# The value product of layer B in plain fp32, two heads side by side in the array's columns

## The chip, the core and the metric

The kernel runs on one core of a Trainium2 chip. The metric is device time in microseconds (us) of one execution. Each compute engine has an instruction stream of its own: TensorE (PE; its weight loads are shown apart as PEld), VectorE (DVE), ScalarE (ACT) and GpSimd (POOL). All transfers of this kernel are issued from SyncE (SP). PE writes its products to PSUM; ACT and DVE read them there; everything else lies in SBUF.

## The reference

Two layers of gated attention over a prompt of 2048 tokens and a sample of 64 tokens, model width 1024, float32 throughout. Layer A has 16 query heads and 2 key/value heads; layer B, where the change is, has 16 heads of 64 columns each. For layer B:

```
h = rms_norm(x, norm_b); q, k, v, gate = split(h @ w_in_b)        # 1024 -> 4 x 1024
q, k = rms_norm per head
s = q k^T / 8 + bias(clipped distance)                            # own chunk of 64 tokens + 8 chunks back
p = softmax(s)
o = p v                                                           # the value product
y = x + (o * silu(gate)) @ w_out_b
```

The sample's 64 tokens attend to 256 cached ones and to themselves. Updated key and value buffers are returned too.

## The kernel before, in words

**Precision.** Large products aren't run in fp32 but in fp32r, a rounded form of it. Each operand is split: a high part (the value rounded to fp32r) and a low part (the value minus its high part). A projection is then three products per weight block: high x high, high x low, low x high. `split_to` (L820) makes such a pair: ACT copies the source into the high part (L822), DVE subtracts (L823).

**Work of layer B.** The prompt is cut into 8 units of 256 tokens (two tiles of 128), the sample is a ninth unit of 64. Heads go in 8 pairs (hp). For each pair and unit, `gen` projects (L529 to L531; the sample L522 to L525), `evacuate` scales the result into SBUF, and `take_vg` hands the values on: `split_v` (L799) writes v's high part by ACT (L801) and its low part by POOL (L802). `VT` holds them for 16 token tiles as [high 64 columns | low 64 columns] per head, `VS` those of the sample.

**Attention of layer B.** For each tile and head, `scores` multiplies queries and keys (L1489, L1490), takes the row maximum with the bias (DVE, L1496) and the exponential (ACT, L1500). `values` (L1519) transposes the probabilities of one tile and head on PE (L850, fp32, against an identity) and splits the result into `ph` and `pl` with `split_to`. `outputs(it, h)` (L1541) is the value product of one head: for each key tile, the stationary operand is the 128 columns [v high | v low] and the moving operand first `ph` (L1566), then `pl` (L1567), added up in PSUM tile `o`. A full unit has four key tiles that all 256 queries see and two that one half sees (128 columns); the first units have fewer. Rows 0 to 63 of `o` then hold high v times p, rows 64 to 127 low v times p. For the second head, `outputs` also transposes the gate on PE, ACT evacuates it (`gate_t`, L1226), and `finish_pairs` (L1229) adds the halves: two ACT copies (L1234), two DVE additions (L1236), a POOL product with the gate (L1237), and a store.

**What sets the order.** PE's order is written out by hand. `pipeline` (L1577) goes through units, and in a unit through four slots (head 0 tile 0, head 0 tile 1, head 1 tile 0, head 1 tile 1). In each slot it emits the scores of this slot, the transposes of the slot before, and, if a head was completed, its value product one slot later. Between these it calls `filler.to(...)`: the filler hands out projection matmuls of later units until a mark is reached, so that PE always has independent work; when layer B's projections are done, it hands out layer B's output projection (L1664 to L1666). The marks count the filler's own columns alone. Work of the other engines is put in a queue (`bg`) with estimated costs and is emitted between; a planner with a simulated timeline orders those engines' streams.

**Fp32 on PE.** Apart from transposes, few fp32 products exist before: the bias vectors (`bias_vectors_a`, L158, 383 columns), and sums of squares against a column of ones (L465, L479).

**Unused code.** `PLAIN = 8` switches off a block scheme for the projections (`block_weights`, `product`, `sums`, `gen_sample`, `gen_blocks`): no head pair reaches it. Its slots in the DRAM cache tensor `xo` stay reserved.

Of the kernel before, what the change touches and what calls it, by code (L numbers as in the profile page):

```python
# [9 lines left out]
F32 = mybir.dt.float32  # L10
# [26 lines left out]
PLAIN = 8  # L37
S_FIRST = (6, 7)
# [17 lines left out]
def hybrid_encoder_kernel(  # L56
# [174 lines left out]
    xo = dr.tile([P, 8 * NU + 1, 8 * P], F32, tag="xo", name="xo")  # L231
# [306 lines left out]
    PIECE = dict(P1="11", P6="T2", P2="21", P7="T3", P5="T1", P4="T4", P3="22")  # L538
    OPERAND = dict(P1="A11", P6="S2", P2="A12", P7="S3", P5="S1", P4="A22", P3="S4")
    SLOT = {n: i for i, n in enumerate(("A11", "A12", "A21", "A22", "S1", "S2", "S3", "S4"))}  # L540

    def block_weights(src):
        w = {n: [Item(), Item()] for n in PIECE.values()}
        raw, todo, emitted = {}, [], []

        def fetch():
            order_ = [(b, a) for b in ("11", "12", "22", "21") for a in range(2)]
            for x, (b, a) in enumerate(order_):
                r = t("wraw", [P, 512], WB) if x < WB else t("xraw", [P, 2 * OT], XR)
                rv = r[:, :512].rearrange("p (k c) -> p k c", k=2)  # L550
                c = 256 * (int(b[1]) - 1)
                held["w"] = load(rv, src[2 * (int(b[0]) - 1) + a][:, :, c : c + 256]).ins
                raw[b, a] = rv

        def g(i, a, j):
            k = 4 * (i - 1) + 2 * a + j
            return gain[:, 1, k : k + 1]

        def piece(n, a, b, scaled):
            def fn():  # L560
                q = w[n][a]
                q.h = wh = t("wh", [P, 1, 512], WN, F32R)[:, 0].rearrange("p (k c) -> p k c", k=2)
                q.l = wl = t("wl", [P, 1, 512], WN, F32R)[:, 0].rearrange("p (k c) -> p k c", k=2)
                rv = raw[b, a]
                if not scaled:
                    nc.scalar.copy(wh, rv)
                    nc.vector.tensor_tensor(wl, rv, wh.bitcast(F32), op=ALU.subtract)
                    return
                for j in range(2):
                    s = g(int(b[0]), a, j)  # L570
                    nc.scalar.activation(wh[:, j], rv[:, j], AF.Identity, scale=s)
                    nc.vector.scalar_tensor_tensor(
                        wl[:, j], rv[:, j], s, wh[:, j].bitcast(F32), op0=ALU.mult, op1=ALU.subtract
                    )
            return 0.8, fn, w[n][a]

        def mix(dst, src_, other, a, op):
            def fn():
                for j in range(2):
                    nc.vector.scalar_tensor_tensor(  # L580
                        raw[dst, a][:, j], raw[src_, a][:, j], g(int(src_[0]), a, j), raw[other, a][:, j],
                        op0=ALU.mult, op1=op,
                    )
            return 0.6, fn, None

        def scaled_12(a):
            def fn():
                for j in range(2):
                    nc.scalar.activation(raw["12", a][:, j], raw["12", a][:, j], AF.Identity, scale=g(1, a, j))
            return 0.6, fn, None  # L590

        two = range(2)
        todo += [piece("11", a, "11", True) for a in two]
        todo += [f(a) for a in two for f in (scaled_12, lambda a: mix("12", "22", "12", a, ALU.subtract))]
        todo += [mix("11", "11", "12", a, ALU.add) for a in two]
        todo += [piece("T2", a, "11", False) for a in two]
        todo += [piece("21", a, "21", True) for a in two]
        todo += [mix("21", "21", "11", a, ALU.subtract) for a in two]
        todo += [piece("T3", a, "12", False) for a in two]
        todo += [mix("11", "22", "11", a, ALU.subtract) for a in two]  # L600
        todo += [piece("T1", a, "11", False) for a in two]
        todo += [piece("T4", a, "21", False) for a in two]
        todo += [piece("22", a, "22", True) for a in two]

        def emit(m=len(todo)):
            if not raw:
                fetch()
            for _ in range(min(m, len(todo))):
                cost, fn, q = todo.pop(0)
                b = bg.put(cost, fn, lazy=filler.n > 0)  # L610
                emitted.append(b)
                if q is not None:
                    q.upto = len(emitted)

        def parts(n, k):
            q = w[n][k // 2]
            for b in emitted[: q.upto]:
                bg.run(b)
            return q.h[:, k % 2], q.l[:, k % 2]

        return parts, emit

    def product(ps, xc, parts, p, start):
        xh, xl = xc.op[OPERAND[p]]
        for k in range(4):
            wh, wl = parts(PIECE[p], k)
            nc.tensor.matmul(ps[:, :256], xh[:, k], wh, start=start and k == 0, stop=False, skip_group_check=not start)
            nc.tensor.matmul(ps[:, :256], xh[:, k], wl, start=False, stop=False, skip_group_check=not start)
            nc.tensor.matmul(ps[:, :256], xl[:, k], wh, start=False, stop=k == 3, skip_group_check=not start)
            if k < 3:  # L630
                yield 3 * 256 / 2400
# [5 lines left out]
    def load_b(unit, hp):  # L637
# [14 lines left out]
        if T == TS:  # L652
            if hp:
                x.joint = cached("J", 8 * NU)[:, : 8 * P].rearrange("p (k s) -> p k s", k=8)
                return x
            raw = t("xraw", [P, 2 * OT], XR)[:, :512].rearrange("p (k s) -> p k s", k=8)
            held["last"] = load(raw, x1[:, :, SEQ:TOK]).ins

            def fn():
                xx = t("xx", [P, 4 * OT], XN, F32R)  # L660
                x.joint = v = xx[:, : 8 * P].rearrange("p (k s) -> p k s", k=8)
                split(xx, v[:, :, :TS], v[:, :, TS:], raw, 8 * NU)

            x.items.append(bg.put(0.52, fn))
            return x
# [11 lines left out]
        def part(n, src, keep):  # L677
            def fn():
                xx = t("xx", [P, 4 * OT], XN, F32R)
                xh, xl = operand(xx)  # L680
                split(xx, xh, xl, raw[src], 8 * u + SLOT[n])
                if keep:
                    x.op[n] = xh, xl
            return fn

        def sums():
            for dst, a, b, op in (
                ("A22", "A21", "A22", ALU.add), ("A21", "A11", "A21", ALU.subtract),
                ("A11", "A22", "A11", ALU.subtract), ("A12", "A12", "A11", ALU.subtract),
            ):  # L690
                def fn(dst=dst, a=a, b=b, op=op):
                    nc.vector.tensor_tensor(raw[dst], raw[a], raw[b], op=op)
                bg.put(0.6, fn)
            for n, src in (("S1", "A22"), ("S3", "A21"), ("S2", "A11"), ("S4", "A12")):
                bg.put(0.52, part(n, src, False))

        if hp == 0:
            raws()
            x.items = [bg.put(0.52, part(n, n, True)) for n in names]
            if u in S_FIRST and PLAIN < 8:  # L700
                sums()
        elif hp < PLAIN:
            for n in names:
                x.op[n] = operand(cached(n, 8 * u + SLOT[n]))
            if u not in S_FIRST and PLAIN < 8:
                raws()
                sums()
        else:
            for n in OPERAND.values():
                x.op[n] = operand(cached(n, 8 * u + SLOT[n]))  # L710
# [120 lines left out]
    def load_cache(ktsrc, vsrc, C, both):  # L831
# [409 lines left out]
    def layer_b():  # L1241
# [4 lines left out]
        def add_unit(hp, unit):  # L1246
# [13 lines left out]
            def weights(*m):  # L1260
                if hp not in st.emit:
                    if hp < PLAIN:
                        (st.w[hp],), _, st.emit[hp] = load_weights(1, (w_in_b[hp], 512))
                    else:
                        st.w[hp], st.emit[hp] = block_weights(w_in_b[hp])
# [40 lines left out]
            def gen_sample():  # L1306
                xc = st.x.pop((hp, u))
                it.prs, it.gate, it.todo = {}, {}, []
                parts = st.w[hp]
                cost = 2 * 256 / 2400  # L1310
                n = TS
# [500 lines left out]
```

## Time and profile before

| what | us |
|---|---|
| median of 3 runs | 2290.27 (2289.32 to 2291.33) |
| the profiled execution, its own time | 2289.07 |
| its span, first to last instruction | 2287.3, mean granted clock of TensorE 0.998 |
| PE busy, all of the span | 2250.9 |
| DVE, ACT, POOL busy | 1539.7, 1466.8, 854.8 |
| 885 to 2072: layer B's attention beside its projections | PE busy 1181.86 of 1187 |
| 2072 to 2130: the rest of it beside the output projection | PE busy 56.60 of 58 |
| 2130 to the end: output projection alone | PE busy 152.53 of 157.3 |

A group row of the profile gives line, engine, operation, tiles (out<-in), array shape (rows * columns of the stationary operand), shape of the moving operand and type, count, then busy time, mean ns of one, and the idle time of the engine just before with what ended it. A timeline row gives start and length in us; merged rows ("x5") give the length of the group. The length of a matmul has a tail that lies under the next one, so lengths don't add up to time; distances between starts do. A wait row gives who waited for whom, the total in us, how many times, and the longest.

### The profile page before, as it was taken

How to read it: one execution, taken by the hardware profiler on the slowest of the kernel's cores; microseconds unless marked ns; L12 is line 12 of the kernel's file. 1: busy time of each engine (PE TensorE's matmuls, PEld its weight loads, DVE VectorE, ACT ScalarE, POOL GpSimd, SP SyncE). 2: the span in 40 equal slices, each digit the busy share in tenths (PEclk: the TensorE clock that was granted, in tenths of full speed). 3: DMA queues.
4: the chain of work that ended last, by engine and by line, in shares of the span. 5: the costliest groups of instructions: out<-in, count | busy, mean ns of one | idle time of the engine just before them, and what ended most of it. 6: DMA issues, size and time to landing. Idle time of an engine off the chain costs nothing. (4 is left out here: it accounts for less than half of the span.)

```text
span 2287.3 us, 41688 instructions
## 1 busy us (share of the span) xinstructions
PE 2250.9 (98%) x13981; PEld 1984.5 (87%) x13981; DVE 1539.7 (67%) x4400; ACT 1466.8 (64%) x3757; POOL 854.8 (37%) x1225
## 2 busy tenths in 40 slices
PE   8999999999999999999999999999999999999999
PEld 7887888888889997888888888888888888888999
DVE  7779888887785545766766766757667667676211
ACT  7888777777773435766666766667667666675321
POOL 5654533333355446442222322322223223234442
PEclk9999999999999999999999999999999999999999
DMA  8846446755437767454454544444445444433664
GB/s 283 296 138 219 161 141 187 227 164 162 147 109 206 213 210 257 160 177 142 150 144 133 156 138 151 136 146 142 142 141 155 138 140 143 137 121 109 194 187 134
DMA packets 236806, 379.31 MB, mean 166 GB/s; under 512 B 24288, under 2 KB 167024, under 8 KB 236560
## 3 DMA queue, kind: packets, MB, share of 16 engines
q1 hardware_dynamic: 236592, 376.65, 53.8%
q8 instruction: 110, 1.80, 0.3%
q14 instruction: 104, 0.85, 0.1%
HBM read 296.13 MB, written 82.08 MB: 165 GB/s over the span
## 5 line engine op out<-in xcount | busy, mean ns | idle before, releaser
L529 PE MATMUL pj<-wh,xx 128*128 128x512 f32 x1024 | 421.9, 412 | 0.0
L531 PE MATMUL pj<-wh,xx 128*128 128x512 f32 x1024 | 403.6, 394 | 0.0
L530 PE MATMUL pj<-wl,xx 128*128 128x512 f32 x1024 | 402.8, 393 | 0.0
L1500 ACT ACTIVATE p<-p,nm 128x640 f32<-128x640 f32 (+5 forms) x272 | 204.2, 751 | 189.4 <-DVE nm L1496 187.7
L1664 PE MATMUL pj<-xx,wh 128*128 128x264 f32 x1024 | 294.4, 288 | 5.2 <-DVE res L1669 5.2
L391 POOL TENSOR_TENSOR xx<-xraw,xx 128x528 fp32r<-128x528 f32 (+1 forms) x168 | 225.1, 1362 | 196.6 <-ACT xx L390 187.1
L1665 PE MATMUL pj<-xx,wh 128*128 128x264 f32 x1024 | 292.0, 285 | 0.0
L1666 PE MATMUL pj<-xx,wl 128*128 128x264 f32 x1024 | 290.6, 284 | 0.0
L823 DVE TENSOR_TENSOR pl<-sb,ph 128x640 fp32r<-128x640 f32 (+5 forms) x272 | 194.8, 716 | 106.0 <-ACT ph L822 102.2
L1496 DVE CUSTOM_DVE_ANT_0 p<-sb,BT 128x640 f32<-128x640 f32 (+5 forms) x272 | 197.0, 724 | 102.0 <-PE sb L1490 99.0
L728 PE MATMUL pj<-wh,xx 128*128 128x512 f32 (+1 forms) x624 | 245.5, 393 | 1.7 <-ACT pb L750 1.2
L729 PE MATMUL pj<-wl,xx 128*128 128x512 f32 (+1 forms) x624 | 232.7, 373 | 2.3 <-DVE wl L320 2.3
L730 PE MATMUL pj<-wh,xx 128*128 128x512 f32 (+1 forms) x624 | 233.4, 374 | 0.0
L531 PEld LDWEIGHTS pj<-wh,xx 128*128 128x128 f32 x1024 | 192.6, 188 | 45.1 <-POOL xx L649 0.4
L1237 POOL TENSOR_TENSOR o<-gt,o 128x256 f32<-128x256 f32 (+2 forms) x140 | 107.8, 770 | 314.8 <-issue 117.9
L822 ACT CAST ph<-sb 128x640 fp32r<-128x640 f32 (+5 forms) x272 | 163.9, 603 | 81.6 <-PE sb L850 76.4
L530 PEld LDWEIGHTS pj<-wl,xx 128*128 128x128 f32 x1024 | 194.1, 190 | 23.1
L529 PEld LDWEIGHTS pj<-wh,xx 128*128 128x128 f32 x1024 | 193.5, 189 | 23.4
L769 POOL TENSOR_TENSOR f<-f,mhalf 128x4 f32<-128x4 f32 (+1 forms) x136 | 137.8, 1013 | 193.6 <-DVE f L768 178.0
L1664 PEld LDWEIGHTS pj<-xx,wh 128*128 128x128 f32 x1024 | 193.5, 189 | 6.8 <-DVE res L1669 6.3
L1666 PEld LDWEIGHTS pj<-xx,wl 128*128 128x128 f32 x1024 | 193.4, 189 | 0.0
L1665 PEld LDWEIGHTS pj<-xx,wh 128*128 128x128 f32 x1024 | 193.2, 189 | 0.2
(222 smaller groups left out, 5658.3 us busy)
## 6 DMA issues: line engine op xcount, KB each, us to landing
xx<-xo SPq DMA_DIRECT2D x231, 512.0 KB, 3.6
xx<-xsa SPq DMA_DIRECT2D x88, 512.0 KB, 4.7
xraw<-oga SPq DMA_DIRECT2D x64, 264.0 KB, 3.5
xo<-xx SPq DMA_DIRECT2D x33, 512.0 KB, 4.7
xraw<-ogb SPq DMA_DIRECT2D x64, 264.0 KB, 3.3
xsa<-xx SPq DMA_DIRECT2D x32, 512.0 KB, 4.2
wraw<-in_w_in_b_dram SPq DMA_DIRECT2D x64, 256.0 KB, 3.5
xraw<-in_x_dram SPq DMA_DIRECT2D x40, 256.0 KB, 4.8
```

Source lines behind the costliest of these rows:

```text
L391: nc.gpsimd.tensor_tensor(xl, rv, xh.bitcast(F32), op=ALU.subtract)
L529: nc.tensor.matmul(ps, xh, wh, start=k == 0, stop=False)
L530: nc.tensor.matmul(ps, xh, wl, start=False, stop=False)
L531: nc.tensor.matmul(ps, xl, wh, start=False, stop=k == KC - 1)
L728: nc.tensor.matmul(ps[:n, :C], xh, wh, start=k == 0, stop=False)
L729: nc.tensor.matmul(ps[:n, :C], xh, wl, start=False, stop=False)
L730: nc.tensor.matmul(ps[:n, :C], xl, wh, start=False, stop=k == KC - 1)
L1496: mi = nc.vector.tensor_tensor_reduce(out=p[:n, :nk], in0=S[:n, o : o + nk], in1=bias[:n, b0 : b0 + nk], op0=ALU.add, op1=ALU.min, scale=1 ...
L1500: ex = nc.scalar.activation(p[:n, :nk], p[:n, :nk], AF.Exp, scale=-1.0, bias=nmh, accum_out=it.sm[:n, 2 * i + h : 2 * i + h + 1],)
L1664: nc.tensor.matmul(ps[:, :OT], wh, oh, start=k == 0, stop=False)
L1665: nc.tensor.matmul(ps[:, :OT], wh, ol, start=False, stop=False)
L1666: nc.tensor.matmul(ps[:, :OT], wl, oh, start=False, stop=k == KC - 1)
```

## The change

The split of values and probabilities in layer B is dropped. V is kept as fp32, 128 columns per token tile for both heads (`value_tiles`, in buffers that layer A's `VT` and `VS` used), copied there by POOL. The transposed probabilities are copied once, as fp32: by ACT for a unit's first tile, by DVE for its second. The value product is one fp32 matmul per key tile and head with that head's 64 columns of v as the stationary operand; `tile_position` puts head 0 into array columns 0 to 63 and head 1 into 64 to 127, and the results into the same rows of PSUM. So both heads share 256 columns of `o`, and there is one product per unit, issued a slot after the last transposes of its second head. With no halves to add, one DVE product of `o` with the gate remains before the store. The two half-seen key tiles come first in the order where there are two. The unused block scheme is removed, and `xo` shrinks to the slots in use. Layer A, projections, scores, softmax and the filler's marks stay.

```diff
-PLAIN = 8
-S_FIRST = (6, 7)
 EARLY = 3
 MORE = 4.7
 WN = 15
...
-    xo = dr.tile([P, 8 * NU + 1, 8 * P], F32, tag="xo", name="xo")
+    xo = dr.tile([P, 4 * NU + 1, 8 * P], F32, tag="xo", name="xo")
 
...
-    PIECE = dict(P1="11", P6="T2", P2="21", P7="T3", P5="T1", P4="T4", P3="22")
-    OPERAND = dict(P1="A11", P6="S2", P2="A12", P7="S3", P5="S1", P4="A22", P3="S4")
-    SLOT = {n: i for i, n in enumerate(("A11", "A12", "A21", "A22", "S1", "S2", "S3", "S4"))}
-
-    def block_weights(src):
-        w = {n: [Item(), Item()] for n in PIECE.values()}
...
+    SLOT = {n: i for i, n in enumerate(("A11", "A12", "A21", "A22"))}
 
...
-    VT = const([P, NT, 2, P], "VT", F32R)
+    VT = t("VT", [P, NT, 2, P], 1, F32R)
     KSA = const([P, CB + TS], "KSA", F32R)
     KSB = const([P, CB + TS], "KSB", F32R)
-    VS = const([P, 3, 2, P], "VS", F32R)
+    VS = t("VS", [P, 3, 2, P], 1, F32R)
+
+    def value_tiles():
+        if "VB" not in held:
+            held["VB"] = t("VT", [P, NT, 2 * HD], 1), t("VS", [P, 3, 2 * HD], 1)
+        return held["VB"]
 
...
+        if both:
+            nc.scalar.copy(value_tiles()[1][:, :nt], rvv.rearrange("p c h d -> p c (h d)"))
+            return
...
             def take_vg(e, v, g):
                 tt, _, n = tiles[e]
-                split_v(n, v[:n], VS[:, 2] if last else VT[:, tt])
+                vb, vs = value_tiles()
+                nc.gpsimd.tensor_copy(vs[:n, 2] if last else vb[:n, tt], v[:n])
...
-                it.p, it.ph, it.pl = {}, {}, {}
+                it.p, it.pt = {}, {}
                 it.base = 0 if last else max(tt - 4, 0)
...
-                it.ph[h] = t("ph", [P, 6, 256], 2, F32R)
-                it.pl[h] = t("pl", [P, 6, 256], 2, F32R)
+                it.pt[h] = t(("ph", "pl")[h], [P, 6, 256], 2)
...
             m = len(sizes)
-            bg.anchor(*split_to(
-                it.ph[h][:, kb : kb + m, t0 : t0 + n], it.pl[h][:, kb : kb + m, t0 : t0 + n], PTv[:, :m, :n],
-            ))
+            copy = (nc.scalar.copy, nc.vector.tensor_copy)[i]
+            bg.anchor(copy(it.pt[h][:, kb : kb + m, t0 : t0 + n], PTv[:, :m, :n]))
             it.sizes = sizes
 
-        def outputs(it, h):
+        def outputs(it):
             u, T, tiles = it.unit
             last = u == NU
-            n = tiles[0][2]
             sizes = it.sizes
-            if h == 0:
-                it.O = psum("o", 512, 1)
-            else:
-                GT = psum("tp", 512, 1)
-                for e, (_, t0, _) in enumerate(tiles):
-                    transpose(GT[:, t0 : t0 + P], it.G[:, e * P : (e + 1) * P])
-                gt = gate_t(GT[:, :T].rearrange("p (j s) -> p j s", j=1), T)
-            mm = []
+            O = psum("o", 512, 1)
+            GT = psum("tp", 512, 1)
+            for e, (_, t0, _) in enumerate(tiles):
+                transpose(GT[:, t0 : t0 + P], it.G[:, e * P : (e + 1) * P])
+            gt = gate_t(GT[:, :T].rearrange("p (j s) -> p j s", j=1), T)
+            vb, vs = value_tiles()
             if last:
-                for c, kn in enumerate(sizes):
-                    mm.append((VS[:kn, c, h], c, kn, 0, TS))
+                mm = [(vs[:, c], c, 0, TS) for c in range(len(sizes))]
             else:
                 ta, tb = tiles[0][0], tiles[1][0]
+                mm = []
+                if ta >= 4:
+                    mm += [(vb[:, ta - 4], ta - 4 - it.base, 0, P), (vb[:, tb], tb - it.base, P, UT)]
                 for kt in range(max(tb - 4, 0), ta + 1):
-                    mm.append((VT[:, kt, h], kt - it.base, P, 0, UT))
-                if ta >= 4:
-                    mm.append((VT[:, ta - 4, h], ta - 4 - it.base, P, 0, P))
-                mm.append((VT[:, tb, h], tb - it.base, P, P, UT))
-            for x, (vt, c, kn, q0, q1_) in enumerate(mm):
-                dst = it.O[:, h * T + q0 : h * T + q1_]
-                nc.tensor.matmul(dst, vt, it.ph[h][:kn, c, q0:q1_], start=x == 0, stop=False)
-                nc.tensor.matmul(dst, vt, it.pl[h][:kn, c, q0:q1_], start=False, stop=x == len(mm) - 1)
-            if h == 1:
-                finish_pairs(
-                    it.O[:, : 2 * T].rearrange("p (j e s) -> p j e s", j=1, e=2),
-                    gt,
-                    T,
-                    og[1][:, it.hp : it.hp + 1, u * UT : u * UT + T],
-                )
-                finished[1, u] = finished.get((1, u), 0) + 1
+                    mm.append((vb[:, kt], kt - it.base, 0, UT))
+                if ta < 4:
+                    mm.append((vb[:, tb], tb - it.base, P, UT))
+            for x, (v, c, q0, q1_) in enumerate(mm):
+                for h, rows in enumerate(halves):
+                    nc.tensor.matmul(
+                        O[rows, q0:q1_], v[:, rows], it.pt[h][:, c, q0:q1_],
+                        start=x == 0, stop=x == len(mm) - 1,
+                        tile_position=(0, rows.start),
+                    )
+            o1 = t("o1", [P, 256])[:, :T]
+            nc.vector.tensor_tensor(o1, O[:, :T], gt[:, 0], op=ALU.mult)
+            store(og[1][:, it.hp, u * UT : u * UT + T], o1)
+            finished[1, u] = finished.get((1, u), 0) + 1
 
...
-                        if prev[1] == len(prev[0].unit[2]) - 1:
-                            nxt = prev[0], prev[2]
+                        if prev[1] == len(prev[0].unit[2]) - 1 and prev[2] == 1:
+                            nxt = prev[0]
                     prev = it, i, h
                     if pend is not None:
-                        outputs(*pend)
+                        outputs(pend)
                     pend = nxt
```

More of the change, by code (lines that the diff above doesn't have):

```diff
@@ L536, in project_b @@
         return cost
-    PIECE = dict(P1="11", P6="T2", P2="21", P7="T3", P5="T1", P4="T4", P3="22")
-    OPERAND = dict(P1="A11", P6="S2", P2="A12", P7="S3", P5="S1", P4="A22", P3="S4")
-    SLOT = {n: i for i, n in enumerate(("A11", "A12", "A21", "A22", "S1", "S2", "S3", "S4"))}
-    def block_weights(src):
-        w = {n: [Item(), Item()] for n in PIECE.values()}
[L544 to L573, printed above, removed]
-                    )
[L575 to L631, printed above, removed]
+    SLOT = {n: i for i, n in enumerate(("A11", "A12", "A21", "A22"))}
@@ L653, in load_b @@
             if hp:
-                x.joint = cached("J", 8 * NU)[:, : 8 * P].rearrange("p (k s) -> p k s", k=8)
+                x.joint = cached("J", 4 * NU)[:, : 8 * P].rearrange("p (k s) -> p k s", k=8)
                 return x
@@ L675, in raws, with part @@
                     raw["A%d%d" % (e + 1, i + 1)] = r
-        def part(n, src, keep):
+        def part(n, src):
             def fn():
@@ L680, in fn @@
                 xh, xl = operand(xx)
-                split(xx, xh, xl, raw[src], 8 * u + SLOT[n])
-                if keep:
-                    x.op[n] = xh, xl
-            return fn
[L686 to L695, printed above, removed]
+                split(xx, xh, xl, raw[src], 4 * u + SLOT[n])
+                x.op[n] = xh, xl
+            return fn
         if hp == 0:
             raws()
[L699 to L702, printed above, removed]
+            x.items = [bg.put(0.52, part(n, n)) for n in names]
+        else:
             for n in names:
[L704 to L707, printed above, removed]
-        else:
-            for n in OPERAND.values():
-                x.op[n] = operand(cached(n, 8 * u + SLOT[n]))
+                x.op[n] = operand(cached(n, 4 * u + SLOT[n]))
         return x
@@ L1261, in weights @@
                 if hp not in st.emit:
[L1262 to L1265, printed above, removed]
+                    (st.w[hp],), _, st.emit[hp] = load_weights(1, (w_in_b[hp], 512))
                 st.emit[hp](*m)
@@ L1304, in gen @@
                     yield c
[L1306 to L1311, printed above, removed]
-                sc = rr[1][:, NT : NT + 1]
-                def run(ps, name, k0, start):
-                    for k in range(4):
-                        wh, wl = parts(name, k)
-                        xk = xc.joint[:, k0 + k]
-                        if start and k == 0:
-                            nc.tensor.matmul(ps[:, :256], xk, wh, start=True, stop=False)
-                        nc.tensor.matmul(
-                            ps[:n, :256], xk[:, :n], wl, start=False, stop=False, skip_group_check=not start
-                        )
-                        if not (start and k == 0):
-                            nc.tensor.matmul(
-                                ps[:, :256], xk, wh, start=False, stop=k == 3, skip_group_check=not start
-                            )
-                        if k < 3:
-                            yield cost
-                A, B = psum("pj", 512, 2), psum("pj", 512, 2)
-                yield from run(A, "11", 0, True)
-                p1 = t("ev", [P, 256], 4)
-                nc.scalar.activation(p1, A[:, :256], AF.Identity, scale=sc)
-                nc.vector.tensor_tensor(p1[:n], p1[:n], p1[n:], op=ALU.add)
-                yield cost
-                yield from run(B, "T1", 0, True)
-                yield cost
-                yield from run(A, "21", 4, False)
-                pr = t("pa", [P, 384], 4)
-                nc.scalar.activation(pr[:, :256], A[:, :256], AF.Identity, scale=sc)
-                nc.vector.scalar_tensor_tensor(
-                    pr[:n, :256], A[:n, :256], sc[:n], pr[n:, :256], op0=ALU.mult, op1=ALU.add
-                )
-                take_qk(0, pr)
-                yield cost
-                yield from run(B, "22", 4, False)
-                vg = t("pb", [P, 256], 6)
-                nc.scalar.activation(vg, B[:, :256], AF.Identity, scale=sc)
-                nc.vector.scalar_tensor_tensor(
-                    vg[:n], B[:n, :256], sc[:n], vg[n:], op0=ALU.mult, op1=ALU.add
-                )
-                nc.vector.tensor_tensor(vg[:n], vg[:n], p1[:n], op=ALU.add)
-                take_vg(0, vg[:, 0:P], vg[:, P : 2 * P])
-                keep_kv(0, vg[:, 0:P])
-                it.ready = True
-                yield cost
@@ L1408, in add_unit @@
-            if T < UT:
-                it.cost = 8 * 2 * 512 / 2400
-            else:
-                it.cost = (8 * 6 * 512 if hp < PLAIN else 7 * 12 * 256) / 2400
-            filler.total += it.cost
+            filler.total += 8 * (6 if T == UT else 2) * 512 / 2400
             it.mark = filler.total
-            filler.add(prefetch, weights if u == 0 else None, gen if hp < PLAIN else gen_blocks if T == UT else gen_sample)
+            filler.add(prefetch, weights if u == 0 else None, gen)
@@ L1579, in pipeline @@
             bg.lazy = True
-            zero(VS[TS:, 2].rearrange("p h d -> p (h d)"))
+            zero(value_tiles()[1][TS:, 2])
             for q in Q2:
@@ L1592, in pipeline @@
                 if x + 2 < len(its):
-                    if its[x + 2].hp >= PLAIN and len(heads) == 4:
-                        end = c0 + 0.875 * PACE_B * len(heads)
                     near = its[x + 2].mark
@@ L1623, in pipeline @@
             filler.to(filler.done + 2.6)
-            if pend is not None:
-                outputs(*pend)
+            assert pend is None
             filler.to(filler.done + 2.6)
-            outputs(prev[0], prev[2])
+            outputs(prev[0])
         return pipeline
```

51 lines of the change are left out of this document (1 added, 50 removed).

## The prediction, made before the changed kernel was run

> **What bounds the kernel now.** I read the page's head first, then the busy time by stage, then the waits of TensorE in layer B (885 to 2130 us, where the changed code runs).
>
> ```profile
> span 2287.3 us, 41688 instructions
> PE 2250.9 (98%) x13981; PEld 1984.5 (87%) x13981; DVE 1539.7 (67%) x4400; ACT 1466.8 (64%) x3757; POOL 854.8 (37%) x1225
> ```
>
> ```profile
> core 0: us, PE busy (x) PEld busy (x) DVE busy (x) ACT busy (x) POOL busy (x), PEclk, DMA share, GB/s
> 1300.00:1500.00 200.00, 199.76 (x1187) 173.16 (x1186) 133.01 (x345) 132.15 (x344) 57.55 (x99) 1.00 0.48 143
> ```
>
> ```profile
> PE sb L850 <- DVE nm L1496: 2.1, 1, 2.1
> PE tp L850 <- DVE KB L1450: 1.8, 2, 1.4
> PE sb L850 <- DVE pl L823: 1.6, 3, 1.2
> PE tp L850 <- ACT gt L1226: 0.7, 1, 0.7
> ```
>
> PE is busy 199.76 of 200 us in a stretch of steady layer B, at clock 1.00, while DVE and ACT are busy two thirds of it and POOL under a third. In all of layer B PE's visible waits sum to 2.1 + 1.8 + 1.6 + 0.7 = 6.2 us. So layer B lasts as long as PE's stream of instructions, and the change is worth what it does to that stream. But busy time has tails that overlap, so the price of a matmul is the distance between starts, which the timeline gives. This is one value product of one head for a full unit (four key tiles of 256 columns and two of 128, twice each), between transposes and projection:
>
> ```profile
> 1501.56 0.71 PE L850 MATMUL sb<-ident,p 128*128 128x128 f32 x5
> ...
> 1502.34 0.28 PE L1566 MATMUL o<-ph,VT 128*128 128x256 f32 x1
> 1502.46 0.28 PE L1567 MATMUL o<-pl,VT 128*128 128x256 f32 x1
> 1502.58 0.28 PE L1566 MATMUL o<-ph,VT 128*128 128x256 f32 x1
> ...
> 1503.12 0.27 PE L1567 MATMUL o<-pl,VT 128*128 128x128 f32 x1
> 1503.23 0.28 PE L1566 MATMUL o<-ph,VT 128*128 128x128 f32 x1
> 1503.34 0.28 PE L1567 MATMUL o<-pl,VT 128*128 128x128 f32 x1
> 1503.45 0.45 PE L529 MATMUL pj<-wh,xx 128*128 128x512 f32 x1
> ```
>
> A 256-column pass follows the last after 0.117 us (1502.34 to 1502.58 is two), a 128-column one after 0.11 to 0.113. That the half-size pass is hardly cheaper says that the 128-column weight load, not the moving columns, sets its pace. A row shows 0.28 because some 0.16 us of tail lies under the next instruction.
>
> **What is removed from PE.** The counts, from the groups by line and shape over the whole run:
>
> ```profile
> L1566 PE MATMUL o<-ph,VT 128*128 128x256 f32 x448 | 122.4, 303 | 0.0
> L1567 PE MATMUL o<-pl,VT 128*128 128x256 f32 x448 | 112.1, 283 | 0.0
> ...
> L1567 PE MATMUL o<-pl,VT 128*128 128x128 f32 x224 | 56.6, 275 | 0.0
> ...
> L1566 PE MATMUL o<-ph,VT 128*128 128x128 f32 x224 | 49.9, 245 | 0.0
> ...
> L1566 PE MATMUL o<-ph,VS 128*128 128x64 f32 x48 | 11.6, 277 | 0.0
> ```
>
> 896 passes x 0.117 = 104.8 us, 448 x 0.113 = 50.6 us, and 96 of the sample unit at about 0.112 = 10.8 us: together **166 us** of PE.
>
> **What is added to PE.** The new product takes fp32 operands instead of fp32r pairs, each head in its own 64 columns: 224 pairs (one matmul per head) of 256 columns, 112 of 128, 24 of 64. The profile of before has one fp32 matmul with many columns, the bias vectors, and it shows how such a call is run:
>
> ```profile
> L158 PE MATMUL tp<-row,tab x2: 480/485/490, 15.4 to 15.8; 32*16 32x383 f32 x2
> ```
>
> ```profile
> 15.09 0.28 PE L729 MATMUL sa<-wl,xx 128*128 128x256 f32 x1
> 15.21 0.28 PE L730 MATMUL sa<-wh,xx 128*128 128x256 f32 x1
> 15.42 0.81 PE L158 MATMUL tp<-row,tab 32*16 32x383 f32 x2
> 16.16 0.50 PE L728 MATMUL pj<-wh,xx 128*128 128x512 f32 x1
> ```
>
> The line runs twice in the whole trace for one call, so a call is two passes. The two end at 15.42 + 0.81 = 16.23; less 0.485 of its own, the second starts at 15.745, 0.325 us after the first: 0.85 ns per column and pass, against 0.117 / 256 = 0.457 ns for fp32r. A call of 256 columns thus takes 2 x 0.217 = 0.435 us, one of 128 columns 0.217.
>
> The number of passes stays the same: 896 + 448 + 96 = 1440 before, (224 + 112 + 24) x 2 heads x 2 passes = 1440 after. Each takes nearly twice as long, but needs only half of the columns. Everything hangs on whether the pass of one head runs **beside** the pass of the other. Nothing in the trace of before does that, so I bound it from both sides:
>
> - Side by side: a pair costs what one call costs. 224 x 0.435 = 97.4, 112 x 0.217 = 24.3; the 24 sample pairs are limited by their four weight loads of 64 columns, 4 x 0.057 = 0.23, so 5.5. Sum 127 us, **39 us less** than 166.
> - One after the other: 194.8 + 48.7 + 5.5 = 249 us, **83 us more**.
>
> The 0.057 is from the sample scores, whose stationary operand is 64 columns wide:
>
> ```profile
> 1012.92 0.22 PE L1489 MATMUL sb<-KSA,q 128*64 128x128 f32 x1
> 1012.98 0.22 PE L1490 MATMUL sb<-KSA,q 128*64 128x128 f32 x1
> 1013.03 0.25 PE L1489 MATMUL sb<-KSA,q 128*64 128x192 f32 x1
> ```
>
> Two 128-column passes in 0.11 us, half of what they cost behind 128-column loads; a 64-column load is therefore no bound on a 128-column fp32 pass of 0.109. I take side by side as the likelier: the two heads write different rows of PSUM, read different weight columns, and the passes are emitted first, second, first, second, so the second pass of one head can always be paired with the first of the other; no data joins them.
>
> The Trainium skill (TensorE: Matmul & The Clock Gate, "Measured speedup vs the span model") reports 2.38x for three column tiles of 32, which also says that they overlap; an estimate by that figure, 2.38/3 of full overlap, would make 127 us into 160, a gain of 6 us. No run here shows it.
>
> **Entering and leaving the narrow form.** There will be 72 groups (one per unit) and so 144 crossings. Two rows bear on the price. The sample projection alternates 64- and 128-column loads with no loss:
>
> ```profile
> 975.01 0.39 PE L525 MATMUL pj<-wh,xx 128*128 128x512 f32 x1
> 975.23 0.39 PE L523 MATMUL pj<-wl,xx 128*64 128x512 f32 x1
> 975.46 0.39 PE L525 MATMUL pj<-wh,xx 128*128 128x512 f32 x1
> ```
>
> The 0.22 and 0.23 us are the ordinary pace. The 32*16 product at 15.42, though, came 0.21 us after a pass that needs 0.12, so 0.09 late, perhaps for a reason of its own. The ends are 0 and, if the pipeline empties, the tail of 0.16 us: 0 to 23 us. I take 0.09, because the fp32 row is nearest in kind: **13 us**.
> The Trainium skill (TensorEngine Tiling (Array Packing), "Key Properties") says that a change of tiling mode drains TensorE; by it the price is the upper end.
>
> **The other engines.** All of this lies beside PE:
>
> ```profile
> L823 DVE TENSOR_TENSOR pl<-sb,ph 128x640 fp32r<-128x640 f32 x192 | 157.9, 822 | 85.6 <-ACT ph L822 81.9
> ...
> L822 ACT CAST ph<-sb 128x640 fp32r<-128x640 f32 x192 | 132.1, 688 | 50.0 <-PE sb L850 45.3
> ...
> L1236 DVE TENSOR_TENSOR o<-o,o 64x256 f32<-64x256 f32 x126 | 52.5, 416 | 37.1 <-ACT o L1234 36.2
> L1237 POOL TENSOR_TENSOR o<-gt,o 128x256 f32<-128x256 f32 x63 | 48.5, 770 | 152.3 <-issue 109.4 <-DVE o L1236 23.4 <-ACT q L1441 17.9
> ```
>
> The transposed probabilities are now copied once, by ACT for the first tile and by DVE for the second, instead of rounded by ACT and subtracted by DVE: about 130 / 2 us off ACT and, at the 822 ns of the subtraction for the copy, 158 / 2 off DVE in the 640-wide form alone. The sum of halves (two ACT copies, two DVE adds, one POOL product per unit) becomes one DVE product of about 0.42 us; POOL's subtraction for v becomes a copy. PE gains at most its waits, 6.2 us; I take 3, since two of the four rows wait for work that stays. If that cover failed, nothing would be lost: every one of these engines has less to do. One wait is new: the product of a unit needs the last copy of its second head, but it is issued a slot of pipeline later, and the copy (0.7 to 0.8 us) replaces a chain of 688 + 822 ns. Behind a late product the projection matmuls on PE would queue. The product also comes once in four slots as one block rather than twice in halves; three slots then come without it, and DVE and ACT, a third free, must keep up with them. I price both at nothing, with the 6 us at stake already in the range. The cache tensor with fewer slots and the removed block code (never called, with PLAIN at 8) move no transfer; V's buffer is taken over from layer A, whose attention is over before the projection of layer B begins.
>
> **Sum.** The profiled execution took 2289.07 us, 1.8 around its span of 2287.3 and 1.2 below the median of 2290.27. 2289.07 - 39 + 13 - 3 = 2260; as a median 2261.
>
> **Rivals**, each from 2290.27.
> - *One after the other* (the case on the other side): the array takes the pass of the second head only when the first has ended, as everything in the trace of before does, and as nothing there contradicts. +83, with the crossings +96, less 3: 2370 to 2383. With a share f of full overlap the product takes 249 - f x 122 us, and with the crossings it may take 166 - 13 + 3 = 156 before the gain is gone: this rival decides below f = 0.76.
> - *Weight loads exposed*: passes overlap, but the load for the other head is taken up only when the pass before it starts, as loads are now:
>
> ```profile
> 1503.74 0.39 PE L530 MATMUL pj<-wl,xx 128*128 128x512 f32 x1
> 1503.74 0.19 PEld L531 LDWEIGHTS pj<-wh,xx 128*128 128x128 f32 x1
> ```
>
> Each of two slots in a pair grows by 0.057: 224 x 0.549 + 112 x 0.331 + 5.5 = 165.6 us, no gain, and crossings on top: 2287 to 2300.
> - *Every crossing empties the pipeline*: side by side, but 144 x 0.16 = 23 us: 2290 - 39 + 23 - 3 = 2271. This is the skill's rule of the drain.
> - *Emptied at every change of head*: in series and 720 changes x 0.16 = 115 us on top: about 2290 + 83 + 115 = 2488.
>
> **How the numbers follow.** Side by side 0.42 (own range 2245 to 2270), with full drains 0.12, one after the other 0.25, loads exposed 0.15, emptied at every change 0.06. Faster by over 0.2% (4.6 us, about what a measurement of this kernel can tell from no change): 0.42 + 0.12 + 0.03 of the exposed case = 0.57; within 0.2%: 0.07; slower: 0.25 + 0.06 + 0.05 = 0.36. The range runs from side by side with free crossings and the whole 6 us (2245) to one after the other with crossings (2385); the last case and small tails stay out.
>
> **What would show it.** In the profile after, the rows of the new product: pairs of starts some nanoseconds apart and a 256-column pair every 0.43 us mean overlap; one every 0.87 us refutes me; 0.55 with loads starting late is the exposed case. The distance from the last transpose to the first pass, and from the last pass to the next projection, gives the crossing. PE's share of waits in layer B should stay under 7 us, with DVE and ACT some 100 us less busy. I am wrong if layer B does not shorten, and the row that says why is that pair distance.

## The result

The changed kernel takes 2262.55 us (median of 4 runs, 2262.1 to 2262.94) where the kernel before takes 2290.8 on the same chip: ratio 0.9878, 95% interval 0.9861 to 0.9895. 2261 was forecast. The head of the page and a stretch of layer B after the change:

```profile
span 2260.3 us, 41004 instructions
PE 2231.6 (99%) x13981; PEld 1908.7 (84%) x13981; DVE 1423.0 (63%) x4168; ACT 1312.7 (58%) x3341; POOL 778.4 (34%) x1153
```

```profile
1300.00:1500.00 200.00, 199.90 (x1212) 163.09 (x1209) 113.00 (x308) 106.70 (x277) 44.43 (x87) 1.00 0.48 144
```

PE's count is the same 13981 as before and it is busy for 199.90 of 200 us: layer B still lasts as long as PE's stream. DVE fell by 116.7 us and ACT by 154.1, and in the stretch they fell to a little over half busy; the time fell by 28. PE's waits between 880 and 2110 us:

```profile
PE tp L743 <- DVE KB L1235: 1.8, 2, 1.4
PE sb L743 <- DVE ph L1321: 0.5, 1, 0.5
PE sb L1274 <- DVE nm L1281: 0.5, 1, 0.5
PE sb L743 <- ACT pb L635: 0.2, 1, 0.2
```

3.0 us in place of 6.2. Over all of layer B, from 855 us to the end, they fell from 9.9 to 3.4 us; 2.8 us of the 9.9 are one wait for DVE at about 880 us, ahead of the first value product. Up to there the changed kernel and experiments 1 to 9 run the same instructions, and yet this wait lasts between 0.3 and 4.7 us in their traces. Where the time went is seen in the timeline of one full unit's product, from the last transpose before it to the projection behind it (start, length, engine, line):

```profile
1494.90 0.38 PE L743 MATMUL tp<-ident,G 128*128 128x128 f32 x2
1495.21 0.32 PE L1347 MATMUL o<-ph,VT 128*64 128x128 f32 x1
1495.22 0.32 PE L1347 MATMUL o<-pl,VT 128*64 128x128 f32 x1
1495.38 0.27 PE L1347 MATMUL o<-ph,VT 128*64 128x128 f32 x1
1495.38 0.27 PE L1347 MATMUL o<-pl,VT 128*64 128x128 f32 x1
...
1495.92 0.38 PE L1347 MATMUL o<-ph,VT 128*64 128x256 f32 x1
1495.92 0.38 PE L1347 MATMUL o<-pl,VT 128*64 128x256 f32 x1
1496.13 0.38 PE L1347 MATMUL o<-ph,VT 128*64 128x256 f32 x1
1496.14 0.38 PE L1347 MATMUL o<-pl,VT 128*64 128x256 f32 x1
...
1497.21 0.38 PE L1347 MATMUL o<-ph,VT 128*64 128x256 f32 x1
1497.22 0.38 PE L1347 MATMUL o<-pl,VT 128*64 128x256 f32 x1
1497.53 0.50 PE L527 MATMUL pj<-wh,xx 128*128 128x512 f32 x1
1497.87 0.39 PE L528 MATMUL pj<-wl,xx 128*128 128x512 f32 x1
```

`ph` is now head 0's tile and `pl` head 1's. Their passes start within 0.01 us of each other, and a pair of passes follows the last after 0.21 to 0.22 us: the heads run side by side, 0.43 us for a key tile of 256 queries and both heads, as the forecast's term has it (0.435). The weight loads in the same place:

```profile
1495.21 0.13 PEld L1347 LDWEIGHTS o<-ph,VT 128*64 128x64 f32 x1 [0.17 <-issue]
...
1495.27 0.14 PEld L1347 LDWEIGHTS o<-ph,VT 128*64 128x64 f32 x1
...
1497.53 0.19 PEld L527 LDWEIGHTS pj<-wh,xx 128*128 128x128 f32 x1 [0.39 <-issue]
```

Within the group each load is early (1495.27 for a pass at 1495.38). At both ends it isn't: the first load of the product starts together with its matmul at 1495.21, and the projection's first load waits until 1497.53, though nothing in the profile is waited for. These are the crossings.

What the rest of the change became, from the groups of layer B by shape:

```profile
L1321 DVE COPY ph<-sb 128x640 f32<-128x640 f32 x48 | 39.6, 825 | 2.5 <-PE sb L743 1.1
...
L1353 DVE TENSOR_TENSOR o<-o,gt 128x256 f32<-128x256 f32 x64 | 27.1, 423 | 88.0 <-PE o L1347 48.1 <-ACT gt L1119 20.3 <-issue 19.2
```

The copy costs DVE the 825 ns that the subtraction cost, but for half of the tiles (this row has those of one head); the one DVE product with the gate takes 423 ns.

**The balance of PE.** Adding up the distances from each pass of the product to the next start on PE gives 171.3 us before and 134.8 after. A group's entry lies ahead of its first pass: the last transpose's distance to it is 0.028 us before (144 groups, 4.1 us) and 0.202 after (72, 14.6). So 175.4 became 149.4, 26.0 us less. But not all of this is gained, because part of it is a transpose's own time, as four rows after the change show:

```profile
1501.07 0.38 PE L743 MATMUL sb<-ident,p 128*128 128x128 f32 x2
1501.21 0.48 PE L527 MATMUL pj<-wh,xx 128*128 128x512 f32 x1
1501.53 0.39 PE L528 MATMUL pj<-wl,xx 128*128 128x512 f32 x1
1501.76 0.39 PE L529 MATMUL pj<-wh,xx 128*128 128x512 f32 x1
```

What follows a last transpose starts 0.028 us behind it and then takes 0.084 longer than elsewhere: a projection matmul 0.315 in place of 0.231, and in the kernel before the first pass of a product 0.202 in place of 0.118. Together this is the 0.11 us in which transposes follow each other. 72 groups of transposes that had a product behind them before have projections or scores behind them after, and this time is paid there: what stands directly behind a transpose or a product takes 7.9 us more than before. The products are thus worth **18.1 us**. The two profiled executions differ by 27.0; the other 9 us lie elsewhere in PE's stream, 6.5 of them as the visible waits named above.

### The profile page after: what moved, and what is told of

Read it like the earlier page. It is cut to its first block, busy times and chain, and to the rows that moved or that the text cites. A ratio compares the mean times of both kernels' runs of the same rounds, so it can differ in the third digit from the quotient of the medians.

```text
span 2260.3 us, 41004 instructions
## 1 busy us (share of the span) xinstructions
PE 2231.6 (99%) x13981; PEld 1908.7 (84%) x13981; DVE 1423.0 (63%) x4168; ACT 1312.7 (58%) x3341; POOL 778.4 (34%) x1153
## 5 line engine op out<-in xcount | busy, mean ns | idle before, releaser
L635 ACT ACTIVATE pa<-pj,rms 128x384 f32<-128x384 f32 (+1 forms) x219 | 118.1, 539 | 136.7 <-PE pj L529 125.8
L388 ACT CAST xx<-xraw 128x528 fp32r<-128x528 f32 (+1 forms) x168 | 103.0, 628 | 133.0 <-PE pj L1443 112.9
L1040 ACT ACTIVATE p<-p,nm 128x257 f32<-128x257 f32 (+2 forms) x272 | 134.5, 497 | 73.5 <-DVE nm L1034 61.3
```

## The experiments

Each starts from the changed kernel, whose ratio to before is 0.9878. All ratios are to runs of the kernel before on the same chip.

**1. All of head 0, then all of head 1**

```diff
-            for x, (v, c, q0, q1_) in enumerate(mm):
-                for h, rows in enumerate(halves):
+            for h, rows in enumerate(halves):
+                for x, (v, c, q0, q1_) in enumerate(mm):
```

> The changed kernel with the loops of its product exchanged: all matmuls of head 0 first, then all of head 1, each head still in its own 64 columns. Theory 1 (TensorE starts its matmuls in the order of the stream, so a pass runs beside another only when its neighbour in the stream lies in the other columns): overlap is lost but for one pass at the border, the product takes 249 instead of 127 us, about 2263 + 122 = 2385 us, and a 256-column pass of one head follows the last after 0.217 us with none beside it. Rival (the two column halves have queues of their own, and each works off its head whatever the order): no change, 2263 us.

2337.85 us, ratio 1.0198 (1.0179 to 1.0218): between the two, 75 us above the changed kernel. Both theories are wrong. The timeline of a full unit ("x9" merges nine passes):

```profile
1023.99 1.73 PE L1347 MATMUL o<-ph,VT 128*64 128x128 f32 x9
1025.35 0.43 PE L1347 MATMUL o<-pl,VT 128*64 128x128 f32 x2
1025.56 0.38 PE L1347 MATMUL o<-ph,VT 128*64 128x256 f32 x1
...
1026.05 1.67 PE L1347 MATMUL o<-pl,VT 128*64 128x256 f32 x7
1027.66 0.50 PE L527 MATMUL pj<-wh,xx 128*128 128x512 f32 x1
```

Head 0 has twelve passes, all ahead of head 1's in PE's program. Eight run alone; at 1025.34 the ninth starts, and head 1's first with it, past passes 10, 11 and 12 that still wait for head 0's columns. Then head 0's last four passes run beside the first six of head 1, of which four are short, and head 1 finishes alone. So TensorE does take later passes ahead of waiting ones, but here only as far as the fourth place behind the pass that it starts. The smallest units (four passes per head) paired up completely: 0.808 us from first pass to next work, 0.801 in the changed kernel.

The Trainium skill (TensorE: Matmul & The Clock Gate, "The mechanism") says that matmuls start strictly in the order of the program; the row at 1025.35, where the thirteenth pass starts before the tenth, disagrees.

**2. Both heads in the same columns**

```diff
...
-                        O[rows, q0:q1_], v[:, rows], it.pt[h][:, c, q0:q1_],
+                        O[0:64, h * T + q0 : h * T + q1_], v[:, rows], it.pt[h][:, c, q0:q1_],
...
-                        tile_position=(0, rows.start),
+                        tile_position=(0, 0),
...
```

The heads follow each other as in experiment 1, and the product with the gate is done for each in turn.

> Both heads in array columns 0 to 63, one head after the other; the results lie side by side in PSUM's free dimension, and two DVE products of 64 rows take the place of one of 128. Same matmuls, same number of passes and of crossings between the 128- and the 64-column form. Theory 1 (the gain is the overlap of the two column halves): no overlap is possible, +122 us, 2385 us. Rival (the gain is fewer operations on DVE, ACT and POOL, and a single fp32 pass is cheap anyway): under 2270 us.

2385.89 us, ratio 1.0421 (1.0398 to 1.0444).

```profile
1505.65 0.38 PE L743 MATMUL tp<-ident,G 128*128 128x128 f32 x2
1505.96 2.38 PE L1347 MATMUL o<-ph,VT 128*64 128x128 f32 x12
1508.17 2.33 PE L1347 MATMUL o<-pl,VT 128*64 128x128 f32 x12
1510.43 0.50 PE L527 MATMUL pj<-wh,xx 128*128 128x512 f32 x1
```

Now 12 passes of one head take 1505.96 to 1508.17, and 12 of the other follow; together 4.47 us where the changed kernel takes 2.31. The overlap is worth 2385.89 - 2262.55 = 123 us (122 expected). Without it the change would have made the kernel 4.2% slower, with DVE, ACT and POOL just as relieved: the rival is out.

**3. Full width, without the narrow form**

```diff
...
-                        O[rows, q0:q1_], v[:, rows], it.pt[h][:, c, q0:q1_],
+                        O[:, h * T + q0 : h * T + q1_], v, it.pt[h][:, c, q0:q1_],
...
-                        tile_position=(0, rows.start),
...
```

> Each head's product runs with all 128 columns of v (both heads') as the stationary operand, so half of every result is left unread; no narrow column form is entered or left. One head after the other, as in the run with both heads in the same columns. Theory 1 with crossings of about 0.33 us per unit (24 us over 72 units, as the trace after the change shows): 2385 - 24 = 2361 us. Rival (the gaps around the product are not those of the narrow form, but of fp32 or of the weights): as slow as with the same columns, 2385 us.

2367.82 us, ratio 1.0334 (1.0319 to 1.035).

```profile
1517.66 0.38 PE L743 MATMUL tp<-ident,G 128*128 128x128 f32 x2
1517.88 2.34 PE L1347 MATMUL o<-ph,VT 128*128 128x128 f32 x12
1520.06 2.34 PE L1347 MATMUL o<-pl,VT 128*128 128x128 f32 x12
1522.04 0.58 PE L527 MATMUL pj<-wh,xx 128*128 128x512 f32 x1
```

The passes are as long as in the narrow form, but the first starts 0.22 us after the row of two transposes, not 0.31, and the projection follows more closely. The times differ by 2385.89 - 2367.82 = 18.1 us. That is not 0.25 us for each of 72 units: in the traces, from the last transpose to the second projection matmul, a prompt unit takes 0.32 to 0.33 us less (4.69 in place of 5.01 for a full one), which makes 20.5 us over the 64 of them, while each of the 8 sample units takes 0.30 more, 2.4 us in all. The sample's passes have 64 columns to move, and at full width they follow each other after 0.112 us, in the narrow form after 0.058. So a way in and out costs what theory 1 says, and the sample, which the expectation had not set apart, takes some of it back.

**4. Twice as many crossings**

```diff
-            for e, (_, t0, _) in enumerate(tiles):
-                transpose(GT[:, t0 : t0 + P], it.G[:, e * P : (e + 1) * P])
-            gt = gate_t(GT[:, :T].rearrange("p (j s) -> p j s", j=1), T)
...
             for x, (v, c, q0, q1_) in enumerate(mm):
+                if x == len(mm) // 2:
+                    for e, (_, t0, _) in enumerate(tiles):
+                        transpose(GT[:, t0 : t0 + P], it.G[:, e * P : (e + 1) * P])
+                    gt = gate_t(GT[:, :T].rearrange("p (j s) -> p j s", j=1), T)
```

> The two transposes of the gate are moved from ahead of the product into its middle, so every unit enters and leaves the 64-column form twice; nothing else is added. Theory 1 (each change between the 128- and the 64-column form empties the pipeline): 72 more entries and exits, +24 us, 2287 us, with a gap of 0.15 to 0.2 us at each. Rival (the gap belongs to the first load of a product or to the wait for its operands): within 5 us of 2263.

2282.11 us, ratio 0.9965 (0.995 to 0.998): 19.6 us more, 0.27 for each added way out and in (here out into transposes, in experiment 3 into a projection).

```profile
1506.25 0.38 PE L1348 MATMUL o<-ph,VT 128*64 128x256 f32 x1
...
1506.57 0.44 PE L743 MATMUL tp<-ident,G 128*128 128x128 f32 x2
1506.93 0.43 PE L1348 MATMUL o<-ph,VT 128*64 128x256 f32 x1
...
1507.20 0.38 PE L1348 MATMUL o<-ph,VT 128*64 128x256 f32 x1
```

The transposes come 0.32 us after a pass that needs 0.22, the product again 0.36 after two transposes that need 0.22, and its first pass then takes 0.27. The gap belongs to the crossing, not to the first load of a unit's product. The rival is out.

**5. The old copies back, on ACT and DVE**

```diff
-            copy = (nc.scalar.copy, nc.vector.tensor_copy)[i]
-            bg.anchor(copy(it.pt[h][:, kb : kb + m, t0 : t0 + n], PTv[:, :m, :n]))
+            dst = it.pt[h][:, kb : kb + m, t0 : t0 + n]
+            bg.anchor(nc.scalar.copy(dst, PTv[:, :m, :n]), nc.vector.tensor_copy(dst, PTv[:, :m, :n]))
```

> The changed kernel with each transposed tile copied twice to the same place, by ACT and then by DVE, which gives these engines the work and the chain of the two steps before the change (688 + 822 ns per 640-wide tile) while PE's stream stays. Theory 1 (beside PE, worth 3 us, at most the 6 us of PE's waits): 2264 to 2269 us. Rival (the relief of ACT and DVE is a main part of the gain, and what the overlap gives is mostly eaten by the crossings): 2275 us or more.

2269.05 us, ratio 0.9899 (0.9882 to 0.9915). Next to 0.9878 (0.9861 to 0.9895) the intervals overlap: by the centres 5 us, 6.5 by the medians, at the upper end of theory 1, but not told from nothing. In the trace the product's distances are those of the changed kernel (135.2 us against 134.8), and PE's visible waits from 855 us on are 8.2 us, 3.4 in the changed kernel. The run brings back the copies alone, not the adding of halves or the split of v. A main part of the gain it is not.

**6. The product ahead of the transposes** (control for 7)

```diff
+                    if pend is not None:
+                        outputs(pend)
                     if prev is not None:
                         values(*prev)
...
-                    if pend is not None:
-                        outputs(pend)
```

> In each slot of the pipeline the value product is emitted before the transposes instead of after them; the control for the run with two units per product. Both theories: within 5 us of 2263.

2260.57 us, ratio 0.9867 (0.9852 to 0.9882): not told from the changed kernel.

**7. Two units per product**

```diff
-                            nxt = prev[0]
+                            done.append(prev[0])
+                            if len(done) == 2:
+                                nxt, done = done, []
...
-        def outputs(it):
+        def outputs(pair):     # transposes and products of both units; unit j in columns UT * j of O
...
```

> The products of two units are emitted as one block (their results side by side in the one PSUM tile, their gate transposes ahead of both), before the slot's transposes; the gate tiles lie in a buffer that layer B leaves unused. Half as many entries and exits of the 64-column form. Theory 1 (0.33 us per pair of crossings): 36 x 0.33 = 12 us less, 2251 us. Rival (the longer block, some 4.5 us in which PE gives the other engines nothing, makes them late, and PE waits for their results): 2263 us or more, with PE's waits in layer B above 10 us.

2254.17 us, ratio 0.9839 (0.9825 to 0.9854), below the changed kernel's interval and the lowest time here with a product of full exactness. By ratios it is 6.4 us under its control (the intervals just touch, but every run is below every run of the control) and 9 under the changed kernel. At the 0.27 us of experiment 4, where the way out also ends in transposes, 36 ways in and out fewer are worth 9.7 us. The longer block costs a little of it:

```profile
PE sb L743 <- DVE ph L1321: 4.4, 4, 1.7
```

That wait was 0.5 us in the changed kernel; all of PE's visible waits from 885 us on are 6.8 us, not the 10 of the rival.

**8. and 9. How far TensorE looks ahead**

```diff
-            for x, (v, c, q0, q1_) in enumerate(mm):
+            for b in range(0, len(mm), 2):          # 3 in the second run
                 for h, rows in enumerate(halves):
...
+                    for x in range(b, min(b + 2, len(mm))):     # 3 in the second run
...
```

> As the changed kernel, but the heads take turns after every two key tiles (four passes of head 0, four of head 1, and so on). The run with the heads apart showed the first pass of head 1 beside the ninth of twelve passes of head 0. Theory 3 (TensorE looks four passes ahead of the one that it starts, past those that wait for busy columns): the first pass of head 1 lies four behind the first of head 0, so all passes still pair up: within 4 us of the changed kernel's 2263 us, all pairs starting together. Rival (the look-ahead is shorter, or counts in another way, for example to the end of the group): 10 us or more slower.

> The same with turns after three key tiles (six passes). Theory 3: head 0 runs two passes alone before head 1's first is within four, and head 1 two at the end: 0.2 to 0.45 us more for each of the 48 full units, 10 to 21 us in all, 2273 to 2284 us; the first pair starts with the third pass. Rival (a look-ahead of six or more passes): 2263 us.

Turns of four passes: 2270.05 us, ratio 0.9904 (0.9887 to 0.9921). All passes pair up, though from the sixth pair on head 1 starts 0.06 us behind head 0, and the sum of the product's distances is 137.7 us against 134.8. Of the other 4 to 5 us above the changed kernel, the profiled execution has 2.5 in the wait at about 880 us ahead of the first product (2.9, in the changed kernel 0.4); the rest stays open, and the runs spread from 2267.1 to 2273.0. The mechanism is as theory 3 has it, the time misses its 4 us. Turns of six passes: 2292.18 us, ratio 1.0002 (0.9991 to 1.0013), a product of 163.1 us:

```profile
1025.22 0.54 PE L1349 MATMUL o<-ph,VT 128*64 128x128 f32 x3
1025.50 0.32 PE L1349 MATMUL o<-pl,VT 128*64 128x128 f32 x1
...
1026.36 0.59 PE L1349 MATMUL o<-ph,VT 128*64 128x256 f32 x2
1026.58 0.43 PE L1349 MATMUL o<-pl,VT 128*64 128x256 f32 x1
```

Head 1 begins beside the third pass of head 0, where theory 3 put it, and a look-ahead of six is excluded. The loss is 0.48 us per full unit, above the 0.2 to 0.45 expected: at 1026.36 head 0 runs one more pass mostly alone, at the border of the next blocks, which I had not counted. The whole gain of the change is gone with it.

**10. Rounded operands in the narrow form**

```diff
-            held["VB"] = t("VT", [P, NT, 2 * HD], 1), t("VS", [P, 3, 2 * HD], 1)
+            held["VB"] = t("VT", [P, NT, 2 * HD], 1, F32R), t("VS", [P, 3, 2 * HD], 1, F32R)
-                it.pt[h] = t(("ph", "pl")[h], [P, 6, 256], 2)
+                it.pt[h] = t(("ph", "pl")[h], [P, 6, 256], 2, F32R)
```

on top of experiment 2.

> As the run with both heads in columns 0 to 63, but probabilities and values are rounded once to fp32r and the low parts are left out, so the value product of layer B is less exact and has one pass for each matmul instead of two. It asks where the gap at the 64-column form comes from: in the projection of the sample (fp32r) 64- and 128-column loads alternated without one. Theory N (any change to the narrow form empties the pipeline here): entry and exit gaps as in the changed kernel, the first pass 0.2 us after the last transpose. Rival (only fp32 in the narrow form does it): 0.11 us, and the projection follows the last pass without a gap. The time is no test of this: by passes (448 x 0.117 + 224 x 0.06 + 48 x 0.06 = 69 us against 135 now) about 2197 us with gaps, 2179 without.

2194.93 us, ratio 0.9577 (0.9563 to 0.9592), with a less exact product.

```profile
1495.54 0.38 PE L743 MATMUL tp<-ident,G 128*128 128x128 f32 x2
1495.68 0.65 PE L1347 MATMUL o<-ph,VT 128*64 128x256 f32 x4
1496.17 0.57 PE L1347 MATMUL o<-pl,VT 128*64 128x256 f32 x4
1496.57 0.45 PE L527 MATMUL pj<-wh,xx 128*128 128x512 f32 x1
```

The product starts 0.14 us after the row of two transposes where experiment 2 needs 0.31: over all groups the distance from the last transpose is 0.028 us, as before the change, not 0.20. Nor is there a gap behind it. The time is 16 us above the 2179 that went with this, and next to the 2197 that went with gaps; the trace has the difference elsewhere. The product's distances sum to 74.2 us, not 69, as each first pass bears its 0.084 us behind a transpose (6 us for 72), and PE's visible waits from 855 us on are 13.9 us, not 3.4. So neither the 64 columns alone (this run) nor fp32 alone (experiment 3) costs a crossing; fp32 in 64 columns does, and fp32r in 128, as in the kernel before, does not. Why, no run here shows.

## Why the prediction was right, step by step

- **What bounds layer B.** Right: PE is as full as before, and the time follows its stream in every run. In experiments 1, 2 and 3 the product's distances and entries grew by 73.5, 123.5 and 101.8 us against the changed kernel, and the time by 75.3, 123.3 and 105.3.
- **Side by side, 39 us less.** Right in kind, and close: about 43. A pair costs 0.43 us as worked out from the bias vectors' fp32 matmul, and overlap against none is 123 us (122 by the two sums). The base of 166 us holds, too: against transposes with a projection straight behind them, the traces price all products at 167 us before and 149 after. Of the 149, 25 are crossings (next point), which leaves 124 for the pairs (127 forecast).
- **Crossings, 13 us.** The mechanism was right, the size about half. The step that failed is the way out, which was priced like the way in. A way in costs 0.14 us in the changed kernel (0.202 in place of 0.109 to the first pass, and 0.16 in place of 0.109 for that pass); a way out costs 0.20 (0.309 in place of 0.216 to the projection, and 0.337 in place of 0.231 for its first matmul). Together this is 0.34 per unit and 25 us for 72, with 0.32 by experiment 3 and 0.27 by experiment 4; that is near the 23 of a full drain, not the 13 taken. The row for the lower end (the sample projection without a loss) was read too widely: it is fp32r, and experiment 10 shows that this makes the difference. The late start of the 32*16 row, which I had let decide, was the better witness, being fp32, but it was read for the way in alone. The drain that the Trainium skill names (TensorEngine Tiling (Array Packing), "Key Properties") is seen here for fp32 in the narrow form, at 0.27 to 0.34 us for a way in and out, and not for fp32r.
- **Other engines, 3 us.** Low: outside the products the two profiled executions differ by 9 us, 6.5 of them in visible waits. How much of this the change causes isn't settled, since 2.4 us are in the wait at about 880 us, which varies by more than that among equal streams; experiment 5 gives 5 to 6.5 for the copies, not told from nothing. Either way it is a side line of a change that takes 117 us off DVE and 154 off ACT.
- **The total was met by luck.** -39 + 13 - 3 = -29 was forecast, about -43 + 25 - 9 = -27 measured: the crossings' error of 12 us is hidden by 4 from the pairs and 6 from the waits.
- **The reason given for overlap** (passes alternate first and second of a call, and the second of one head pairs with the first of the other) was wrong. The heads' first passes start together at 1495.21, past head 0's second, because TensorE looks ahead. The number came out alike, since either pairing fills both halves.
- **The rivals.** *One after the other* is what happens with the columns or the order chosen otherwise: its price, +83 to +96, is met by experiment 2's 2385.89 - 2290.56 = 95. *Loads exposed* is out: loads within the group start a pass early, and a 256-column pair takes 0.43 us, not 0.55. *Emptied at every change of head* is out: pairs start 0.01 us apart. *Full drains* had the price of the crossings right: 25 us measured, 23 by this rival. Its total of 2271 is too high because it shared the other two terms, which gained 10 us more than they were taken at.

## What to carry to other kernels

Where a kernel is bound by TensorE, price a rewrite of a product in passes times distance between starts, with the way into the group and the way out of it each priced for itself, and take each distance from a row of the same type: here the fp32r rows misled on the crossing. Before calling a sum of distances a gain, see that what stands behind the neighbours has not grown: 7.9 of 26.0 us were only moved. Two products of 64 columns run side by side only if the program brings them within about four passes of each other; taking turns every matmul is the safe order, and turns of three matmuls lost the whole gain. Gather fp32 products in the narrow form into few long groups, since each way in and out cost 0.27 to 0.34 us here.

## What I had not expected of the hardware

TensorE starts a pass ahead of earlier ones that wait for their columns: the thirteenth of 24 beside the ninth, and with turns of six passes the seventh beside the third. Both fit a reach of four places; the runs don't show what is counted (passes or loads and passes). And the gap at the narrow form is tied to fp32: 0.27 to 0.34 us for a way in and out in fp32, none in fp32r of the same 64 columns, none in fp32 of 128.
